# Two-operand elementwise operations moved from GpSimd to VectorE in a hybrid mLSTM and attention step

## The chip, the cores and the metric

The kernel runs on one core of one Trainium2 chip. The metric is the device time of one execution in microseconds, as the median of several runs.

## The reference

One layer of a decoder for a prompt of 1024 tokens and 32 sample tokens (8 sequences of 4), model width 1024, all in float32. Two branches read the same normalised input and are merged by gates:

```
h, gate = adaln_in(x, c, w_ada, b_ada, g_norm)          # rmsnorm(x) * (1 + scale) + shift
(mq, mk, mv, mi, mf, mo, mz, aq, ak, av, az, gm, ga) = split_in(h @ w_in)
y_m, C, n, m = mlstm_branch(mq, mk, mv, mi, mf, mo, mz, C0, n0, m0, b_i, b_f, g_mn)
q = partial_rope(aq, pos); k = partial_rope(ak, pos)
o = attn_prompt(q, k, v, sinks)                          # window 128, 8 heads, 2 key heads
y_a = o * silu(az)
u = sigmoid(gm) * (y_m @ w_mo) + sigmoid(ga) * (y_a @ w_ao)
x = x + gate * (u @ w_o)                                 # then a last rmsnorm
```

Inside the mLSTM branch, for each of 4 heads and each chunk of 128 tokens (b is the running sum of the log forget gates):

```
dmat = where(causal, b[:, None] - b[None, :] + ig[None, :], -inf)
s = (q @ k.T) * exp(dmat - m_hat[:, None])
num = s @ v + w_inter[:, None] * (q @ C)
h = num / max(abs(dot), exp(-m_hat))[:, None]
C_new = decay * C + (w_end * k).T @ v
```

and its output is multiplied by sigmoid(mo) * silu(mz). The sample tokens take the same layer with a state C0, n0, m0 of their own and cached keys and values.

## The kernel before

**Engines by name.** In the code V is VectorE (DVE in the profile), S is ScalarE (ACT), G is GpSimd (POOL); every load and store is issued on SyncE's queue (SP). V and S are wrappers that record each instruction, so that all their work, and TensorE's, has one helper line in the profile: L219 for V and S, L257 for products (`mm`), L262 for transposes (`tr`), L245 for transfers. G is the bare engine, so that its instructions carry the line of the code that issues them.

**Products.** A float32 product is three reduced-precision ones: an operand is split into hi (a cast, on ScalarE) and lo = raw - hi (a subtraction, on VectorE), and hi x hi, hi x lo and lo x hi are added in PSUM. Tokens are columns, in pieces of 384, 384 and 288 (1024 prompt and 32 sample tokens).

**Stages.** From 0 to about 60 us the input is loaded and normalised. To about 360 us follow the projections ("jobs"): attention queries, then for each mLSTM head its queries, keys and values (tiles g_aq, g_mq, g_mk, g_mv). Between their products TensorE is given pieces of side work by a planner that keeps a clock of estimated product times: attention units (scores sc, exponentials p, transposes pt, ScalarE's and VectorE's copies of them pT, output oT), the gate chain, and the heads in stages a to d. From 360 to 690 us come the gates' projections in 14 pairs of weights (8 `gate`, 2 `query_gate`, 4 `head_gate`), each pair by a scheme with seven block products instead of eight, for which sums of blocks of the input (`sum_blocks`, tiles hb) and of the weights (`Pair.first_sums`, `Pair.split`, tiles wr_ and ws) are made ahead. Splits of weights (tiles wh_, wl_) are made two products ahead. Then follow the two branches' output products (g_w_ao, g_w_mo) and the last product (fo).

**Rope** (line 737). A tile x of queries or keys becomes x * cos + shuffle(x) * sin: VectorE shuffles and multiplies by sin (ropet), the other product is a second instruction, VectorE adds both (aqr, krr).

**Head stage a** (lines 1029 and 1032). Tile et is loaded with rows of the gate chain and the causal mask is added; tile qw is loaded with weights and multiplied by the head's queries hq. A memset of vn's last column (line 1022) is on GpSimd too, with ScalarE's weighting hv <- vn behind it.

**Other names.** f3den, f3v, f3r_ and f2...: the small chain (3 or 2 columns) that normalises a head's chunk outputs, ending in a scaling of et; mx, nmx, den: the softmax's maximum, its negative, its denominator; gs: the sample tokens' head output times a weight; row: a row of the gate chain; t1 to t4 with h and l: splits of the hb sums; bx, by, bz, bw: PSUM banks of the block products, evacuated into gt, zt or hg; ho: a head's or query's output that hg or zt is multiplied by (lines 1416 and 1392); Cs: the sample states, decayed at line 1174; sU: the products that update them; uqv, ukv: loaded attention operands.

**What sets the order.** TensorE's order is fixed by hand: each product is made to follow the one before it (`in_order`). VectorE and ScalarE are ordered by hand in the beginning only; from there on a scheduler orders VectorE, ScalarE, GpSimd and SyncE by its own estimates. Each engine then takes its instructions strictly in that order, each waiting for its own operands.

## Time and profile before

| | |
|---|---|
| median of 3 runs | 882.72 us (882.6 to 884.04) |
| profiled execution | 881.87 us |
| its span | 880.1 us |
| TensorE (PE) busy | 844.3 us, 96% |
| VectorE (DVE) busy | 546.8 us, 62% |
| ScalarE (ACT) busy | 383.9 us, 44% |
| GpSimd (POOL) busy | 200.6 us, 23%, 206 instructions |
| HBM traffic | 106.02 MB read, 39.51 MB written |

Times are microseconds from the start of the span unless marked ns. A row of a timeline gives the start, the duration, the engine, the line, the operation, the tile written, the tiles read, the shape and a count; in brackets stands the engine's idle time just before it and what ended it. A row of a group gives busy time in all and the mean of one instruction in ns. An idle engine costs time only if something that sets the end waits for it.

### The profile page before, as it was taken

How to read it: one execution, taken by the hardware profiler on the slowest of the kernel's cores; microseconds unless marked ns; L12 is line 12 of the kernel's file. 1: busy time of each engine (PE TensorE's matmuls, PEld its weight loads, DVE VectorE, ACT ScalarE, POOL GpSimd, SP SyncE). 2: the span in 40 equal slices, each digit the busy share in tenths (PEclk: the TensorE clock that was granted, in tenths of full speed). 3: DMA queues.
4: the chain of work that ended last, by engine and by line, in shares of the span. 5: the costliest groups of instructions: out<-in, count | busy, mean ns of one | idle time of the engine just before them, and what ended most of it. 6: DMA issues, size and time to landing. Idle time of an engine off the chain costs nothing. (4 is left out here: it accounts for less than half of the span.)

```text
span 880.1 us, 15550 instructions
## 1 busy us (share of the span) xinstructions
PE 844.3 (96%) x5304; PEld 715.1 (81%) x5304; DVE 546.8 (62%) x1512; ACT 383.9 (44%) x984; POOL 200.6 (23%) x206
## 2 busy tenths in 40 slices
PE   6899999999999889999999999999999999999996
PEld 2689988888889878788878877777788999987775
DVE  4877673444748876444754554567756667747785
ACT  4762344445445455555545444444344333223231
POOL 0002320000024432223312223355443302220000
PEclk9899999999999999999999999999999999999998
DMA  9996437374567443445444344554424789453421
GB/s 312 369 332 199 117 123 266 106 239 128 172 176 225 141 141 109 128 150 149 100 137 119 107 128 122 155 160 134 132 85 140 256 279 304 141 156 106 145 79 48
DMA packets 114347, 145.55 MB, mean 165 GB/s; under 512 B 27068, under 2 KB 72508, under 8 KB 114236
## 3 DMA queue, kind: packets, MB, share of 16 engines
q1 hardware_dynamic: 114268, 144.56, 52.0%
q8 instruction: 42, 0.69, 0.3%
q14 instruction: 37, 0.30, 0.1%
HBM read 106.02 MB, written 39.51 MB: 165 GB/s over the span
## 5 line engine op out<-in xcount | busy, mean ns | idle before, releaser
L257 PE MATMUL g_w_ao<-ya,wh_w_ao 128*128 128x384 f32 (+1 forms) x192 | 45.5, 322 | 0.9 <-ACT bw L219 0.5
L257 PE MATMUL g_w_mo<-ym_l,wh_w_mo 128*128 128x384 f32 (+1 forms) x192 | 45.7, 323 | 0.0
L219 ACT ACTIVATE p<-p,nmx 128x256 f32<-128x256 f32 (+1 forms) x64 | 31.0, 485 | 30.1 <-DVE nmx L219 30.1
L219 DVE CUSTOM_DVE_ANT_0 p<-sc,cst,sink 128x256 f32<-128x256 f32 (+1 forms) x64 | 26.1, 462 | 21.6 <-PE sc L257 21.5
L257 PEld LDWEIGHTS g_w_ao<-ya,wh_w_ao 128*128 128x128 f32 x192 | 33.4, 188 | 1.6 <-ACT bw L219 1.0
L219 ACT ACTIVATE fjk<-rows_l 128x512 bf16<-128x512 f32 (+2 forms) x19 | 11.6, 609 | 51.7 <-DVE rows_l L219 25.8
L257 PEld LDWEIGHTS g_w_mo<-ym_l,wh_w_mo 128*128 128x128 f32 x192 | 33.5, 188 | 0.0
L257 PE MATMUL g_mk<-h_h,wh_mk 128*128 128x384 f32 (+1 forms) x96 | 33.4, 348 | 0.0
L257 PE MATMUL g_aq<-h_h,wh_aq 128*128 128x384 f32 (+1 forms) x96 | 33.0, 344 | 0.0
L257 PE MATMUL g_mv<-h_h,wh_mv 128*128 128x384 f32 (+1 forms) x96 | 33.0, 344 | 0.0
L257 PE MATMUL g_mq<-h_h,wh_mq 128*128 128x384 f32 (+1 forms) x96 | 32.5, 338 | 0.0
L257 PE MATMUL g_aq<-h_l,wh_aq 128*128 128x384 f32 (+1 forms) x96 | 31.6, 329 | 0.0
L257 PE MATMUL g_aq<-h_h,wl_aq 128*128 128x384 f32 (+1 forms) x96 | 31.6, 329 | 0.0
L257 PE MATMUL g_mk<-h_l,wh_mk 128*128 128x384 f32 (+1 forms) x96 | 31.6, 329 | 0.0
L257 PE MATMUL g_mk<-h_h,wl_mk 128*128 128x384 f32 (+1 forms) x96 | 31.4, 327 | 0.0
L257 PE MATMUL g_mv<-h_h,wl_mv 128*128 128x384 f32 (+1 forms) x96 | 31.0, 323 | 0.0
L257 PE MATMUL g_mq<-h_l,wh_mq 128*128 128x384 f32 (+1 forms) x96 | 31.0, 323 | 0.0
L257 PE MATMUL g_mq<-h_h,wl_mq 128*128 128x384 f32 (+1 forms) x96 | 31.0, 323 | 0.0
L257 PE MATMUL g_mv<-h_l,wh_mv 128*128 128x384 f32 (+1 forms) x96 | 31.0, 323 | 0.0
L257 PE MATMUL g_w_mo<-ym_l,wl_w_mo 128*128 128x384 f32 (+1 forms) x96 | 31.0, 323 | 0.0
L257 PE MATMUL g_w_ao<-ya,wl_w_ao 128*128 128x384 f32 (+1 forms) x96 | 30.8, 321 | 0.0
L737 POOL TENSOR_TENSOR aq<-aq,cos 128x384 f32<-128x384 f32 (+1 forms) x12 | 15.0, 1252 | 46.1 <-DVE ropet L219 40.2
(1321 smaller groups left out, 2746.1 us busy)
## 6 DMA issues: line engine op xcount, KB each, us to landing
x<-xT SPq DMA_DIRECT2D x16, 256.0 KB, 5.2
early_h<-w_ada SPq DMA_DIRECT2D x8, 512.0 KB, 7.7
hD<-x SPq DMA_DIRECT2D x16, 256.0 KB, 4.8
adar_ga<-w_ada SPq DMA_DIRECT2D x16, 256.0 KB, 5.4
wr_ga<-w SPq DMA_DIRECT2D x16, 256.0 KB, 3.1
hb<-hD SPq DMA_DIRECT2D x16, 256.0 KB, 6.5
wr_gm<-w SPq DMA_DIRECT2D x16, 256.0 KB, 3.3
taD<-gt SPq DMA_DIRECT2D x16, 256.0 KB, 3.4
```

The source lines that it names most:

```text
L219: ins = f(*args, **kw)
L257: in_order(nc.tensor.matmul(out, lhsT, rhs, start=start, stop=stop, skip_group_check=more))
L737: G.tensor_tensor(x, x, cs[0], op=ALU.mult)
```

## The change

Every `G.tensor_tensor` in six places becomes a `V.tensor_tensor` with the same operands: rope's cosine product, the mask and the weighting of head stage a, the decay of the sample states, the block sums, the weight sums, and the last multiplication of the two kinds of gated outputs. That is 139 instructions.

```diff
 def rope(x, cs, n, dst, dram, c0):
-            G.tensor_tensor(x, x, cs[0], op=ALU.mult)
+            V.tensor_tensor(x, x, cs[0], op=ALU.mult)
...
 def stage_a(p):
-                G.tensor_tensor(et[:, :m], et[:, :m], cmask.unsqueeze(1).to_broadcast((128, m, 128)), op=ALU.add)
+                V.tensor_tensor(et[:, :m], et[:, :m], cmask.unsqueeze(1).to_broadcast((128, m, 128)), op=ALU.add)
...
-                G.tensor_tensor(qw[:, :m], qw[:, :m], q[:, :w].rearrange("p (c e) -> p c e", e=128), op=ALU.mult)
+                V.tensor_tensor(qw[:, :m], qw[:, :m], q[:, :w].rearrange("p (c e) -> p c e", e=128), op=ALU.mult)
...
 for c, b, m in zip(Cs, bs, ns_):
-                G.tensor_tensor(c[:, :m], c[:, :m], sxb[:, h, 2, b].unsqueeze(2).to_broadcast((128, m, 129)), op=ALU.mult)
+                V.tensor_tensor(c[:, :m], c[:, :m], sxb[:, h, 2, b].unsqueeze(2).to_broadcast((128, m, 129)), op=ALU.mult)
...
 def sum_blocks():
-                G.tensor_tensor(b22, b22, b12, op=ALU.subtract)
+                V.tensor_tensor(b22, b22, b12, op=ALU.subtract)
...
 def first_sums(self):
-                G.tensor_tensor(self.raw["s1"], self.raw[1, 0], self.raw[1, 1], op=ALU.add)
+                V.tensor_tensor(self.raw["s1"], self.raw[1, 0], self.raw[1, 1], op=ALU.add)
...
 def split(self, i):
-                    G.tensor_tensor(r[0, 1], r[0, 1], r[0, 0], op=ALU.subtract)
+                    V.tensor_tensor(r[0, 1], r[0, 1], r[0, 0], op=ALU.subtract)
...
 query_gate.evac
-                G.tensor_tensor(t, t, self.held.pop((c, th)), op=ALU.mult)
+                V.tensor_tensor(t, t, self.held.pop((c, th)), op=ALU.mult)
...
 head_gate.evac
-                    G.tensor_tensor(z, z, self.held.pop(th), op=ALU.mult)
+                    V.tensor_tensor(z, z, self.held.pop(th), op=ALU.mult)
```

The other three block sums and two first sums change in the same way. Left on GpSimd are its memsets, small copies of sample columns (line 976), the lo parts of ya and of half of wo (lines 1700 and 1723) and the output additions of line 1244.

TensorE's order stays the same, row for row. VectorE's order takes in the new instructions where the scheduler puts them. In rope, on VectorE (the last query piece), the cosine product stands behind the sine product, and a weight split comes ahead of the addition:

```order
 L219 STREAM_SHUFFLE ropet<-aq 128x288
 L219 TENSOR_TENSOR ropet<-ropet,sin_545 128x288
-L219 TENSOR_TENSOR den<-den,nmx 128x4
+L219 TENSOR_TENSOR aq<-aq,cos_544 128x288
+L219 TENSOR_TENSOR wl_mk_1_1517<-wr_mk_1_1286,wh_mk_1_1516 128x512
 L219 TENSOR_TENSOR aqr<-aq,ropet 128x256
 L219 TENSOR_TENSOR qpad<-aq,ropet 64x8x4 x2
-L219 TENSOR_TENSOR wl_mk_1_1517<-wr_mk_1_1286,wh_mk_1_1516 128x512
+L219 TENSOR_TENSOR den<-den,nmx 128x4
```

So a cosine product is now followed by the addition on the same engine; the softmax's den moves behind it.

On VectorE near the first block sums (hb_0, at 262 us in the profile before), two score passes (the rows with ISA write mx) stand ahead:

```order
 L219 ISA p_3167,mx<-sc_6_1_3170,cst,sink 128x256
 L219 ISA mx 128x1
-L219 SCALAR_TENSOR_TENSOR fsden<-sns 32x1
+L219 TENSOR_TENSOR hb_0_3134<-hb_0_3134,hb_0_3130 128x512
 L219 TENSOR_SCALAR nmx<-mx 128x4
 L219 TENSOR_TENSOR nmx<-sink,mx 128x4
+L219 TENSOR_TENSOR hb_0_3130<-hb_0_3130,hb_0_3128 128x512
+L219 SCALAR_TENSOR_TENSOR fsden<-sns 32x1
```

The first sum, which reads a tile that a load has to bring, stands ahead of nmx now.

On VectorE near the second block sums (hb_1, at 281 us), where gs stood near the end of the f3 chain:

```order
+L219 TENSOR_TENSOR hb_1_3376<-hb_1_3376,hb_1_3382 128x512
 L219 RECIPROCAL f3den<-f3den 128x3
+L219 TENSOR_TENSOR hb_1_3380<-hb_1_3380,hb_1_3376 128x512
 L219 TENSOR_TENSOR f3v<-f3den 128x3
+L219 TENSOR_TENSOR t4l_3244<-hb_0_3132,t4h_3243 128x512
+L219 COPY mk_3494<-g_mv_3424 128x384
+L219 TENSOR_TENSOR et<-et,cst 128x256
+L219 TENSOR_TENSOR qw<-qw,hq_2_3160 128x256
+L219 TENSOR_SCALAR gs<-sty_3513,vec 128x32
 L219 TENSOR_TENSOR f3v<-f3v,mssq 128x3
```

t4l, the mk copy and gs move ahead of the rest of the chain (they leave its end), and et and qw come in just ahead of gs.

GpSimd's queue at the same place, before:

```order
L1279 TENSOR_TENSOR hb_1_3382<-hb_1_3382,hb_1_3378 128x512
L1280 TENSOR_TENSOR hb_1_3378<-hb_1_3378,hb_1_3376 128x512
L1330 TENSOR_TENSOR ws_4245<-wr_gm_0_3951,wr_gm_1_3953 128x512
L1282 TENSOR_TENSOR hb_1_3376<-hb_1_3376,hb_1_3382 128x512
L1283 TENSOR_TENSOR hb_1_3380<-hb_1_3380,hb_1_3376 128x512
L1022 MEMSET vn 128x2
L1029 TENSOR_TENSOR et<-et,cst 128x256
L1032 TENSOR_TENSOR qw<-qw,hq_2_3160 128x256
L1022 MEMSET vn 128x3
```

and after, from the copy of sample columns ahead of it:

```order
L976 COPY ks<-mk_3389 128x32
L1022 MEMSET vn 128x2
L1022 MEMSET vn 128x3
L976 COPY vs<-mk_3662 128x32
L976 COPY qs<-mk_3944 128x32
```

The memset of vn, which ScalarE waits for, has no sum ahead of it any more.

More of the change, by code (lines that the diff above doesn't have):

```diff
@@ L1278, in sum_blocks @@
                     block_tiles(n, k)
-                G.tensor_tensor(b22, b22, b12, op=ALU.subtract)
-                G.tensor_tensor(b12, b12, b11, op=ALU.subtract)
+                V.tensor_tensor(b22, b22, b12, op=ALU.subtract)
+                V.tensor_tensor(b12, b12, b11, op=ALU.subtract)
                 yield 2.5, ""
-                G.tensor_tensor(b11, b11, b22, op=ALU.add)
-                G.tensor_tensor(b21, b21, b11, op=ALU.subtract)
+                V.tensor_tensor(b11, b11, b22, op=ALU.add)
+                V.tensor_tensor(b21, b21, b11, op=ALU.subtract)
                 t1.append(b12)
@@ L1329, in first_sums @@
                 self.raw["s1"] = raw_tile("ws1")
-                G.tensor_tensor(self.raw["s1"], self.raw[1, 0], self.raw[1, 1], op=ALU.add)
-                G.tensor_tensor(self.raw[1, 0], self.raw[0, 0], self.raw[1, 0], op=ALU.subtract)
-                G.tensor_tensor(self.raw[0, 0], self.raw["s1"], self.raw[0, 0], op=ALU.subtract)
+                V.tensor_tensor(self.raw["s1"], self.raw[1, 0], self.raw[1, 1], op=ALU.add)
+                V.tensor_tensor(self.raw[1, 0], self.raw[0, 0], self.raw[1, 0], op=ALU.subtract)
+                V.tensor_tensor(self.raw[0, 0], self.raw["s1"], self.raw[0, 0], op=ALU.subtract)
             def split(self, i):
```

## The prediction

> **What bounds the kernel now.** I read the page's shares first, then the chain, then TensorE's waits, and last the timelines around those waits.

> ```profile
> PE 844.3 (96%) x5304; PEld 715.1 (81%) x5304; DVE 546.8 (62%) x1512; ACT 383.9 (44%) x984; POOL 200.6 (23%) x206
> PE 31%; issue 1%; DVE 1%; POOL 1%; DMA 1%; SPq 0%; ACT 0%; POOLq 0%; DVEq 0%
> ```

> TensorE is busy 96% of the span, and GpSimd (POOL) makes 1% of the chain that ended last. The change takes no instruction from TensorE, so all it can win is TensorE's waits and what they do to its clock. TensorE's waits (line, tile, engine waited for: us in total, times, longest), without those of the first and last 60 us and three under 0.7 us:

> ```profile
> PE bw L257 <- ACT bw L219: 2.8, 2, 1.6
> PE sc L257 <- ACT uqv L219: 2.6, 1, 2.6
> PE pt L262 <- DVE gs L219: 2.5, 1, 2.5
> PE sU L257 <- DVE Cs L219: 2.5, 4, 0.9
> ...
> PE pt L262 <- DVE row L219: 1.9, 1, 1.9
> ...
> PE smp L257 <- ACT pT L219: 0.9, 1, 0.9
> ...
> PE g_w_ao L257 <- POOL ya L1700: 0.4, 1, 0.4
> ```

> Together 13.6 us. To these come two stretches at half clock (columns: window, length, TensorE busy, granted clock), the first behind the wait for row, the second behind that for uqv:

> ```profile
> 115.77:119.18 3.41, 3.41 (x13) 0.50 0.00 0
> 327.39:330.81 3.42, 3.42 (x11) 0.50 0.22 77
> ```

> Half of 3.41 us, 1.7 us, is the most that each can cost; I take 1.6. So 13.6 + 3.2 = 16.8 us (1.9%) is the ceiling of a gain here.

> **What moves.** 139 two-operand instructions leave POOL for VectorE (DVE): 88 of 512 columns, 26 of 384, 8 of 387, 8 of 256, 4 of 258, 5 of 288, some 62,700 columns, or 122 x 512. DVE's price for such a product, and a DVE group of the same size that runs beside POOL:

> ```profile
> L219 DVE TENSOR_TENSOR wl_mk<-wr_mk,wh_mk 128x512 fp32r<-128x512 f32 x8 | 5.5, 690 | 2.3 <-ACT wh_mk L219 2.2
> L219 DVE SCALAR_TENSOR_TENSOR hg<-hg,hg 128x512 f32<-128x512 f32 x8 | 11.4, 1423 | 0.2
> ```

> 122 x 0.69 = 84 us of new DVE work. Against it stands what DVE loses beside POOL: 8 x (1.42 - 0.69) = 5.9 us in the hg group alone. It shows best on three-column instructions:

> ```profile
> 281.80 1.29 POOL L1279 TENSOR_TENSOR hb<-hb,hb 128x512 f32<-128x512 f32 x1 [3.33 <-DVE f3den L219]
> 281.91 1.20 DVE L219 TENSOR_TENSOR f3v<-f3den 128x3 f32<-128x3 f32 x1
> 288.24 0.10 POOL L1022 MEMSET vn<- 128x2 f32 x1
> 288.37 0.70 ACT L219 ACTIVATE hv<-vn,wend 128x129 f32<-128x129 f32 x2 [6.07 <-POOL vn L1022]
> 289.87 0.16 DVE L219 TENSOR_TENSOR f3r_w<-f3r_w,f3v 128x3 f32<-128x3 f32 x1
> 291.22 0.24 DVE L219 TENSOR_SCALAR gs<-sty,vec 128x32 f32<-128x32 f32 x1
> ```

> f3v, started behind hb, ends with hb, near 283.1; alone such an instruction takes 0.16 us. [...] From rows, DVE ends between 547 (all 84 us given back) and 547 + 84 - 6 = 625 us; I take the middle, 585 (66%). DVE does not become full, so the question is place by place, in DVE's order.

> 1. **Rope, 107 to 115 us.** DVE waits for POOL's cosine product, and TensorE for DVE's copy `row`, which stands behind it:

> ```profile
> 111.17 1.08 POOL L737 TENSOR_TENSOR aq<-aq,cos 128x288 f32<-128x288 f32 x1 [2.27 <-DMA qD<-aqr]
> 112.30 0.42 DVE L219 TENSOR_TENSOR aqr<-aq,ropet 128x256 f32<-128x256 f32 x1 [0.71 <-POOL aq L737]
> 114.92 0.55 PE L262 MATMUL pt<-cst,p 128*128 128x128 f32 x3 [1.87 <-DVE row L219]
> ```

> On DVE this product costs 0.69 x 288/512 = 0.4 us and the wait of 0.71 goes: 0.3 us earlier, and 0.35 more from the rope before it. The stall shrinks by 0.65 to 1.2 us. Waits of that length elsewhere (bw, 1.2 and 1.6) had no half-clock stretch behind them, so its 1.6 us go too: -2.2.

> 2. **Block sums hb_1, 281 to 291 us** (rows above). POOL's five products hold back the `vn` memset, that holds ACT for 6.07 us, and they stretch DVE's chain, behind which stands `gs`. After, the sums cost DVE 5 x 0.69 = 3.5 us, but et, qw and gs stand ahead of most of that chain. From 281.05: products 3.5, two C updates 0.7, small ones 0.65, t4l 0.7, the mk copy 0.55, et and qw 0.9: gs starts near 288 instead of 291.2, before TensorE comes to pt: -2.5.

> 3. **Block sums hb_3, 321 to 340 us.** POOL waits for the tile's DMA beside DVE; after the change DVE itself waits, with the attention's `nmx` behind it:

> ```profile
> 321.90 0.16 DVE L219 TENSOR_TENSOR f2v<-f2den 128x2 f32<-128x2 f32 x1
> 325.06 1.26 POOL L1279 TENSOR_TENSOR hb<-hb,hb 128x512 f32<-128x512 f32 x1 [3.86 <-DMA hb<-hD]
> 325.34 0.62 ACT L219 CAST t2h<-hb 128x512 fp32r<-128x512 f32 x1 [2.68 <-DMA qD<-mk]
> 328.05 2.73 DVE L219 TENSOR_SCALAR et<-et,f2den,f2r_y 128x128 f32<-128x128 f32 x2
> 333.04 0.17 DVE L219 TENSOR_SCALAR nmx<-mx 128x4 f32<-128x4 f32 x1
> L219 DVE CUSTOM_DVE_ANT_0 p<-sc,cst,sink 128x256 f32<-128x256 f32 (+1 forms) x64 | 26.1, 462 | 21.6 <-PE sc L257 21.5
> ```

> DVE arrives at 321.9 and blocks 3.2 us, but the two et scalings, 2.73 us under POOL, stand behind nmx now. From 325.06: four sums 2.8, t2l and t4l 1.4, four score passes 1.85, small ones 1: nmx near 332.1, 0.9 us earlier. The wait of smp for pT (0.9) goes: -0.9. The 2.6 us for uqv stay, since ACT ahead of it waits for a DMA, and so does the half clock behind them.

> 4. **Gate evacuation, 439 us.**

> ```profile
> 438.01 0.35 DVE L219 TENSOR_SCALAR et<-et,f3den,f3r_y 128x128 f32<-128x128 f32 x1
> ...
> 438.87 1.56 DVE L219 TENSOR_SCALAR et<-et,f3den,f3r_y 128x128 f32<-128x128 f32 x2
> 439.03 1.32 POOL L1339 TENSOR_TENSOR wr_ga<-wr_ga,wr_ga 128x512 f32<-128x512 f32 x1 [1.67 <-DVE wl_pgate__5310 L219]
> ```

> The weight sum costs the two et 0.9 us, and with them gt, ACT's bw copy and TensorE (1.6) are late. After, DVE pays 0.69 for it, and et and qw just ahead no longer stretch two small instructions: -0.6, between -1.6 and 0.

> 5. **ya, 691 us.** The last ya product stood on POOL behind an hg product:

> ```profile
> 689.13 1.45 POOL L1416 TENSOR_TENSOR hg<-hg,ho 128x512 f32<-128x512 f32 x1 [0.63 <-DVE hg L219]
> ```

> With hg gone from POOL's queue ya starts up to 1.4 us earlier: -0.4. (Six ya, eight wo_l and six output adds stay on POOL; the diff does not touch them.)

> 6. **Losses.** DVE takes its instructions in order, so a sum that waits for a DMA holds all behind it. The worst is hb_0, with `nmx` next:

> ```profile
> 262.79 0.08 DVE L219 DVE_READ_ACCUMULATOR2_ANT mx<- 128x1 f32 x1
> 264.75 0.15 DVE L219 TENSOR_SCALAR nmx<-mx 128x4 f32<-128x4 f32 x1
> 266.61 1.29 POOL L1279 TENSOR_TENSOR hb<-hb,hb 128x512 f32<-128x512 f32 x1 [8.73 <-DMA n_s<-Cs]
> 271.01 0.91 ACT L219 ACTIVATE p<-p,den 128x256 f32<-128x256 f32 x2 [2.92 <-DVE den L219]
> ```

> DVE comes to it at 262.9 and can start near 266.5; nmx moves to 267.3, 2.5 us later. What covers it: ACT's four exponentials then end 2.5 us later, at 269.7, while the step after them waits now until 271.0 for a den that stands in DVE's stretched chain. I charge 0.3, between 0 and 2.5. et and qw hold DVE in the same way near 198 us (0.4) and 245 (0.2). The decay of Cs brings DVE three products a head in the sample stage, where TensorE waits 0.6 us a head for Cs: they run 0.2 us apiece faster or slower than now, -2.4 to +2.4 in all; I take +0.5. Weight splits fall behind et and qw once or twice; they are made two products ahead, and these cover them: 0; without that cover the wait is that of an et for its DMA, up to 4 us. A few stores change places with loads on SP's queue; their readers come a product later: 0 to 0.5, taken as 0. Sum +1.4, at worst some +5.

> Sum: -2.2 - 2.5 - 0.9 - 0.6 - 0.4 + 1.4 = -5.2 us. The profiled execution takes 881.87 (span 880.1), which makes 876.7; the median of the runs shown, 882.72, lies 0.85 higher: 877.5.

> **Rivals.**

> - *TensorE alone sets the time; no change.* Each wait above ends on the next thing: at 114.9 on the score passes, at 291 on ACT's pT, at 340 on the softmax. For it: 96% busy, and the sum is 0.6% of the time. Against it: gs, row and Cs are DVE's with POOL in front of it. 881 to 884.5.

> - *DVE blocked at its head: slower.* One mechanism, the in-order wait for a DMA that POOL took until now; it decides where the 2.5 us at hb_0 and the 3.2 us at hb_3 exceed the softmax's lead over TensorE's pt. With no lead at both: 2.5 + 3.2 and two half-clock stretches, +8.9, less places 1, 4, 5 and half of 2 (4.4): 887.2. Against it: TensorE idles little there, so its leads are mostly long:

> ```profile
> 180.00:360.00 180.00, 172.47 (x1275) 154.64 (x1274) 117.03 (x362) 93.51 (x284) 44.59 (x55) 0.99 0.56 168
> ```

> - *The clock stays.* A wait's length alone does not bring the half clock: 2.5 us before 291.5 did not, 1.9 before 114.9 did. If the first stretch stays, 879.1. [...]

> - *More goes than I count.* uqv's 2.6 us and its stretch go too: 877.5 - 4.2 = 873.3. Against it: ACT's DMA wait at 325.34.

> **How the numbers follow.** Forecast with either clock case (875.5 to 880.9) 0.57; more goes (below 875.5) 0.11; no change 0.18; blocked DVE 0.14. A measurement of this kernel tells some 0.2% (1.8 us) from no change: faster 0.68, same 0.18, slower 0.14. The predicted time is **877.5 us**. The range leaves out the end of the last rival (0.05) and the blocked DVE: 873.5 to 884.5; the forecast's own is 875.5 to 880.9.

> **What will show it.** Right: DVE near 585 us; the f3v chain at 0.16 us apiece; no TensorE wait for gs, and the one for row near 1.2 us with no half clock behind it; none for ya. Wrong: TensorE waits for ACT's yt, pT or p near 200 or 265 to 275 us while DVE stands ahead of hb, et or qw for a DMA; new half-clock stretches; weight splits later than their products.

## The result and the profile after

The changed kernel takes 869.66 us (median of 4 runs, 868.19 to 870.61) against 882.66 us for the kernel before (median of 4 runs, 880.67 to 884.04): a ratio of 0.9853, with an interval of 0.9829 to 0.9877. That is 13.0 us faster where 5.2 were forecast, and below the range's end of 873.5. The direction and most places were right; the step that failed is place 3, with the wait for uqv.

The page of the profiled execution after (870.61 us, span 868.8; shares of the span, then the chain that ended last):

```profile
PE 842.2 (97%) x5304; PEld 712.6 (82%) x5304; DVE 569.3 (66%) x1651; ACT 385.0 (44%) x984; POOL 33.3 (4%) x67
PE 56%; DVE 2%; ACT 1%; issue 0%; DVEq 0%
```

139 instructions went from POOL (206 to 67) to DVE (1512 to 1651), and POOL is gone from the chain. DVE rose by 22.5 us only. In this trace the 139 add 75.1 us to its busy time (569.3 with them, 494.2 without them; their own times add up to 87.6 us, but neighbouring instructions overlap: at 264.94, below, nmx starts 0.08 us before the sum ahead of it ends), and the other 1512 take 494.2 us instead of 546.8: 52.6 us came back. TensorE's waits after, the same view as before:

```profile
PE sU L257 <- DVE Cs L219: 3.7, 4, 1.4
...
PE bw L257 <- ACT bw L219: 2.0, 2, 1.2
...
PE sc L257 <- ACT uqv L219: 0.2, 1, 0.2
PE pt L262 <- DVE row L219: 0.2, 1, 0.2
PE smp L257 <- ACT pT L219: 0.2, 1, 0.2
```

No wait is left for gs (2.5), none for ya (0.4); row fell from 1.9 to 0.2, uqv from 2.6 to 0.2, smp from 0.9 to 0.2; sU grew by 1.2. TensorE's busy time within the stretch that held the long waits, which was 172.47 of 180 us:

```profile
180.00:360.00 180.00, 176.37 (x1301) 158.41 (x1298) 117.93 (x416) 99.42 (x301) 4.49 (x19) 1.00 0.59 172
```

Its granted clock is 1.00 now, and between 60 and 860 us no stretch at half clock is left, where there were two.

**An account by place.** TensorE runs the same 5304 instructions in the same order in both kernels, so the start of one instruction in both traces gives a lag, and the steps of the lag say where the time went. With before's times:

| where (before's time) | step, us | what |
|---|---|---|
| first 60 us | +0.5 | loads of x and of the gates; -2.3 to +2.2 in the runs below |
| 112 to 119, place 1 | -3.2 | wait for row -1.67, half clock -1.53 |
| 256, sample stage | +0.8 | wait for Cs |
| 291.5, place 2 | -2.7 | wait for gs |
| 326.7, place 3 | -4.0 | wait for uqv -2.43, its half clock -1.54 |
| 332 and 340, place 3 | -1.4 | waits for mx and pT, small steps between |
| 442.8, place 4 | -0.8 | wait for bw |
| 577.9, sample stage | +0.5 | wait for Cs |
| 691.4, place 5 | -0.6 | wait for ya |
| the rest | -0.4 | steps under 0.3 us each |
| all | -11.3 | 881.87 to 870.61 us |

The profile after is the slowest of its four runs, and the first 60 us (-2.3 to +2.2) and single waits (up to 1.6 us, in the second execution of the kernel before) differ between runs, so the 1.7 us between -11.3 and the medians' -13.0 are not put to a place.

**Place 1.** Timeline after: the addition of one rope (107.82), then the next rope with its product by cos, then TensorE's transpose behind row:

```profile
107.82 0.56 DVE L219 TENSOR_TENSOR aqr<-aq,ropet 128x384 f32<-128x384 f32 x1
...
110.67 0.45 DVE L219 TENSOR_TENSOR aq<-aq,cos 128x288 f32<-128x288 f32 x1
111.15 0.42 DVE L219 TENSOR_TENSOR aqr<-aq,ropet 128x256 f32<-128x256 f32 x1
...
113.78 0.55 PE L262 MATMUL pt<-cst,p 128*128 128x128 f32 x3 [0.20 <-DVE row L219]
```

**Place 2.** The f3 chain after, gs and the transpose that waited for it:

```profile
282.34 0.15 DVE L219 TENSOR_TENSOR f3v<-f3den 128x3 f32<-128x3 f32 x1
...
284.15 0.24 DVE L219 TENSOR_SCALAR gs<-sty,vec 128x32 f32<-128x32 f32 x1
...
286.53 0.88 PE L262 MATMUL pt<-cst,p 128*128 128x128 f32 x6
```

f3v takes 0.15 us instead of 1.20, and gs is done 2.1 us before TensorE comes to pt.

**Place 3, the step that was wrong.** Before, ACT's cast `t2h` waited 2.68 us for a store (qD<-mk), and I took that as a DMA's own time. SyncE's queue and DVE before:

```profile
306.38 1.62 POOL L1280 TENSOR_TENSOR hb<-hb,hb 128x512 f32<-128x512 f32 x1
306.77 1.25 DVE L219 TENSOR_SCALAR nmx<-mx 128x4 f32<-128x4 f32 x1
...
317.37 2.81 SPq L245 DMA_DIRECT2D hb<-hD  x4
320.85 0.32 SPq L245 DMA_DIRECT2D qD<-mk  x1
```

and after, with the cast and TensorE's score product behind it:

```profile
301.46 0.16 DVE L219 TENSOR_SCALAR nmx<-mx 128x4 f32<-128x4 f32 x1
...
309.06 3.92 SPq L245 DMA_DIRECT2D hb<-hD  x4
...
315.60 0.32 SPq L245 DMA_DIRECT2D qD<-mk  x1
...
317.47 0.62 ACT L219 CAST t2h<-hb 128x512 fp32r<-128x512 f32 x1
...
319.58 1.13 PE L257 MATMUL sc<-ukv,uqv 64*128 64x256 f32 x6 [0.21 <-ACT uqv L219]
```

Before, the four hb_3 loads (1 MB) were issued right ahead of the small store: 0.67 us lie between the end of their issue and the store's. By the landing events of the trace the last load landed at 324.90 and the store at 325.27, 4.42 us after its issue; t2h started at 325.34. After, the gap is 2.62 us, the last load landed at 316.08, and the store at 317.39, 1.79 us after its issue; t2h started at 317.47, after a wait of 0.04 us. The loads are issued 8.3 us sooner (3.6 of it against TensorE, whose lag is 4.7 there), since the work ahead of them on SyncE's queue is: before, `nmx` at 306.77 took 1.25 us instead of 0.16 beside POOL's hb_2 sums, and behind it came ACT's exponentials, a copy of mk and the store of that copy, which stands ahead of the loads. The scheduler also put that copy of mk ahead of the scaling by den, so the timeline does not say how much of the 8.3 us each of the two brought.

**The loss at hb_0 came as told, and was covered.** After, DVE, then ACT:

```profile
264.33 0.69 DVE L219 TENSOR_TENSOR hb<-hb,hb 128x512 f32<-128x512 f32 x1 [3.35 <-DMA hb<-hD]
264.94 0.16 DVE L219 TENSOR_SCALAR nmx<-mx 128x4 f32<-128x4 f32 x1
...
267.85 0.91 ACT L219 ACTIVATE p<-p,den 128x256 f32<-128x256 f32 x2
```

DVE stands 3.35 us ahead of the sum, with nmx behind it. The exponentials begin late (nmx 2.1 us later against TensorE), yet the scaling by den starts at 267.85 instead of 271.01, 1.3 us sooner against TensorE: den stood behind three instructions of one column that took 1.14 to 1.15 us beside POOL's sums; now they take 0.15, and den stands ahead of them. TensorE is busy 20.00 of 20 us from 260 to 280 in both kernels.

### The profile page after: what moved, and what is told of

Its sections match the earlier page's. It is cut to its first block, busy times and chain, and to the rows that moved or that the text cites. A ratio compares the mean times of both kernels' runs of the same rounds, so it can differ in the third digit from the quotient of the medians.

```text
span 868.8 us, 15418 instructions
## 1 busy us (share of the span) xinstructions
PE 842.2 (97%) x5304; PEld 712.6 (82%) x5304; DVE 569.3 (66%) x1651; ACT 385.0 (44%) x984; POOL 33.3 (4%) x67
## 4 chain that ended last, share of the span: by engine, by line
PE 56%; DVE 2%; ACT 1%; issue 0%; DVEq 0%
PE fo L257 10%; PE bw L257 9%; PE bx L257 9%; PE by L257 9%; PE g_w_mo L257 5%; PE g_w_ao L257 5%; PE bz L257 4%; PE smp L257 2%; PE n L257 1%; PE S L257 0%; PE U L257 0%; PE sn L257 0%; PE smpo L257 0%; PE ty L262 0%; DVE rows_l L219 0%
## 5 line engine op out<-in xcount | busy, mean ns | idle before, releaser
L257 PE MATMUL g_w_ao<-ya,wh_w_ao 128*128 128x384 f32 (+1 forms) x192 | 45.3, 321 | 0.5 <-ACT bw L219 0.5
L257 PE MATMUL g_w_mo<-ym_l,wh_w_mo 128*128 128x384 f32 (+1 forms) x192 | 45.7, 323 | 0.0
L219 ACT ACTIVATE p<-p,nmx 128x256 f32<-128x256 f32 (+1 forms) x64 | 30.9, 484 | 22.6 <-DVE nmx L219 22.6
L219 DVE CUSTOM_DVE_ANT_0 p<-sc,cst,sink 128x256 f32<-128x256 f32 (+1 forms) x64 | 26.4, 462 | 15.0 <-PE sc L257 15.0
L219 ACT ACTIVATE fjk<-rows_l 128x512 bf16<-128x512 f32 (+2 forms) x19 | 11.6, 609 | 51.3 <-DVE rows_l L219 25.5
L257 PEld LDWEIGHTS g_w_ao<-ya,wh_w_ao 128*128 128x128 f32 x192 | 33.3, 188 | 1.0 <-ACT bw L219 1.0
L257 PEld LDWEIGHTS g_w_mo<-ym_l,wh_w_mo 128*128 128x128 f32 x192 | 33.5, 188 | 0.0
L257 PE MATMUL g_mv<-h_h,wh_mv 128*128 128x384 f32 (+1 forms) x96 | 33.0, 344 | 0.0
L257 PE MATMUL g_mk<-h_h,wh_mk 128*128 128x384 f32 (+1 forms) x96 | 32.8, 341 | 0.0
L257 PE MATMUL g_mq<-h_h,wh_mq 128*128 128x384 f32 (+1 forms) x96 | 32.5, 338 | 0.0
L257 PE MATMUL g_aq<-h_h,wh_aq 128*128 128x384 f32 (+1 forms) x96 | 32.3, 336 | 0.0
L257 PE MATMUL g_mv<-h_h,wl_mv 128*128 128x384 f32 (+1 forms) x96 | 31.0, 323 | 0.0
L257 PE MATMUL g_mq<-h_h,wl_mq 128*128 128x384 f32 (+1 forms) x96 | 31.0, 323 | 0.0
L257 PE MATMUL g_mk<-h_l,wh_mk 128*128 128x384 f32 (+1 forms) x96 | 31.0, 323 | 0.0
L257 PE MATMUL g_mq<-h_l,wh_mq 128*128 128x384 f32 (+1 forms) x96 | 31.0, 323 | 0.0
L257 PE MATMUL g_aq<-h_l,wh_aq 128*128 128x384 f32 (+1 forms) x96 | 31.0, 323 | 0.0
L257 PE MATMUL g_mv<-h_l,wh_mv 128*128 128x384 f32 (+1 forms) x96 | 31.0, 323 | 0.0
L257 PE MATMUL g_mk<-h_h,wl_mk 128*128 128x384 f32 (+1 forms) x96 | 31.0, 323 | 0.0
L257 PE MATMUL g_w_mo<-ym_l,wl_w_mo 128*128 128x384 f32 (+1 forms) x96 | 31.0, 323 | 0.0
L257 PE MATMUL g_aq<-h_h,wl_aq 128*128 128x384 f32 (+1 forms) x96 | 31.0, 323 | 0.0
L257 PE MATMUL g_w_ao<-ya,wl_w_ao 128*128 128x384 f32 (+1 forms) x96 | 30.8, 321 | 0.0
L219 DVE SCALAR_TENSOR_TENSOR u_h<-tgw_ao,g_w_ao 128x384 f32<-128x384 f32 (+1 forms) x24 | 12.4, 518 | 13.2 <-PE g_w_ao L257 13.0
```

Source lines behind the costliest of these rows:

```text
L219: ins = f(*args, **kw)
L257: in_order(nc.tensor.matmul(out, lhsT, rhs, start=start, stop=stop, skip_group_check=more))
```

## The experiments

Theory A of the expectations is the prediction's mechanism, with what the trace after added: DVE's small instructions take longer beside POOL's two-operand ones (f3v 1.20 us beside a block sum before, 0.15 after); TensorE's waits for row and gs follow from that at once, and the wait for uqv one step later, by way of SyncE's queue. Its rivals stand in the texts themselves. Ratios are to the kernel before on the same chip in the same series (881.89 us there for the first four).

### The rope alone (15 of 139 instructions)

```diff
-            G.tensor_tensor(x, x, cs[0], op=ALU.mult)
+            V.tensor_tensor(x, x, cs[0], op=ALU.mult)
```

> Only rope's 15 cosine products go to VectorE. Theory A (the gain is made at separate places, each by its own group): TensorE's wait for row at 114.9 us falls from 1.87 us to 0.7 or less and the half-clock stretch at 115.8 us (1.5 to 1.7 us) goes, nothing else changes: 2.5 to 3.3 us faster than before. Theory B (the gain needs GpSimd empty everywhere, since the groups hand their delays on to each other): under 1 us, and the stretch at half clock stays or moves.

Measured: 879.71 us, ratio 0.997 (0.9953 to 0.9988). The timeline at place 1:

```profile
115.47 0.55 PE L262 MATMUL pt<-cst,p 128*128 128x128 f32 x3 [0.20 <-DVE row L219]
```

The wait falls from 1.87 to 0.20 us and no half clock follows: -3.2 us by the lag, the whole of place 1. The medians give 2.2 us (1.1 to 4.1 by the interval), a little under the 2.5 to 3.3 expected. uqv (2.7) and gs (2.7) stay. The wait for bw at 442 shrinks from 1.57 to 0.89 though nothing near it was changed; this returns below.

### The block sums alone (16 instructions)

```diff
-                G.tensor_tensor(b22, b22, b12, op=ALU.subtract)
-                G.tensor_tensor(b12, b12, b11, op=ALU.subtract)
+                V.tensor_tensor(b22, b22, b12, op=ALU.subtract)
+                V.tensor_tensor(b12, b12, b11, op=ALU.subtract)
...
-                G.tensor_tensor(b11, b11, b22, op=ALU.add)
-                G.tensor_tensor(b21, b21, b11, op=ALU.subtract)
+                V.tensor_tensor(b11, b11, b22, op=ALU.add)
+                V.tensor_tensor(b21, b21, b11, op=ALU.subtract)
```

> Only the 16 block sums hb go to VectorE. Theory A: TensorE's wait for gs (2.5 us) goes, and with the sums off GpSimd at 305 to 311 us the softmax, ScalarE's mk copy and SyncE's loads of hb_3 come 2 to 3 us earlier against TensorE, so that the store of mk lands before ScalarE wants its buffer: the wait for uqv (2.6 us), its half-clock stretch (1.7) and most of the wait for pT (0.9) go too: 7 to 9 us faster. Theory B (the wait for uqv is a DMA's own, as the prediction had it, and was cured by something else in the change): 3 to 4 us faster, the wait for uqv still 2 us or more.

Measured: 873.0 us, ratio 0.9898 (0.9869 to 0.9927). Sixteen instructions bring nearly 9 us. gs -2.70, uqv -2.43 and its half clock, mx and pT about -1.4; the wait for row and its half clock stay. The queue, the cast and the product at place 3:

```profile
311.40 3.03 SPq L245 DMA_DIRECT2D hb<-hD  x4
...
316.49 0.32 SPq L245 DMA_DIRECT2D qD<-mk  x1
...
318.35 0.62 ACT L219 CAST t2h<-hb 128x512 fp32r<-128x512 f32 x1
...
320.53 1.13 PE L257 MATMUL sc<-ukv,uqv 64*128 64x256 f32 x6 [0.21 <-ACT uqv L219]
```

2.06 us between the loads and the store, which lands 1.78 us after its issue. So moving the block sums is enough to take the wait for uqv away.

### The weight sums alone (56 instructions)

```diff
-                G.tensor_tensor(self.raw["s1"], self.raw[1, 0], self.raw[1, 1], op=ALU.add)
+                V.tensor_tensor(self.raw["s1"], self.raw[1, 0], self.raw[1, 1], op=ALU.add)
...
-                    G.tensor_tensor(r[0, 1], r[0, 1], r[0, 0], op=ALU.subtract)
+                    V.tensor_tensor(r[0, 1], r[0, 1], r[0, 0], op=ALU.subtract)
```

(lines 1331 and 1332 likewise)

> Only the 56 sums of weights go to VectorE. Theory A: TensorE's wait for bw at 442.8 us shrinks by about 0.8 us, the rest stays: 0.5 to 1 us faster. Theory B (what matters is how much work GpSimd has in all; these are 40% of it): 4 us or more faster.

Measured: 882.39 us, ratio 1.0017 (1.0002 to 1.0031): no gain, where A had a small one. bw -0.73 at 442, but Cs at 578 +0.49, and the wait for gs is 3.6 instead of 2.5 us, now with half clock behind it. The largest group of moved instructions is worth nothing; how much work leaves POOL does not set the gain.

### The rest alone (masks, weightings, decay, gating: 52 instructions)

```diff
-                G.tensor_tensor(et[:, :m], et[:, :m], cmask.unsqueeze(1).to_broadcast((128, m, 128)), op=ALU.add)
+                V.tensor_tensor(et[:, :m], et[:, :m], cmask.unsqueeze(1).to_broadcast((128, m, 128)), op=ALU.add)
```

(lines 1032, 1174, 1392 and 1416 likewise)

> Masks, weightings, state decays and the two kinds of gated outputs (52 instructions) go to VectorE. Theory A: the wait for ya (0.4 us) goes, part of bw's wait perhaps, and the waits for Cs grow by 1.2 us in all: within 1 us of before. Theory B (GpSimd's amount of work counts): 4 us or more faster.

Measured: 883.83 us, ratio 1.0026 (1.0006 to 1.0047): 1.9 us slower, where A had it within 1 us. Waits of TensorE:

```profile
PE sU L257 <- DVE Cs L219: 4.2, 4, 2.0
PE pt L262 <- DVE gs L219: 2.9, 1, 2.9
PE n L257 <- DVE mx L219: 2.6, 1, 2.6
...
PE sc L257 <- ACT uqv L219: 0.2, 1, 0.2
```

uqv is cured here too, which neither theory had (the store is issued 1.51 us behind the loads and lands at 323.72, 1.90 us later), and a wait of 2.6 us for mx, which was 0.2, stands in its place 6 us later. Taking uqv's wait away brought nothing here, where POOL still has the block sums; how DVE's chain behind it runs beside them (1.11 to 1.25 us for instructions of 0.16) is shown by the run with the whole change but for the block sums, below.

### The hb_3 loads issued behind the store

Everything stays on POOL; only the last block load is issued after the transfer that follows it.

```diff
-                if k < 3:
+                if k < 2:
                     nxt = load(k + 1)
...
+                    if k == 2 and n == "t3":
+                        nxt = load(3)
```

> The kernel before, all sums on GpSimd; only the four loads of hb_3 are issued one transfer later on SyncE's queue, behind the store of mk that ScalarE's t2h waits for. Theory A (that store lands late because 1 MB of loads is queued just ahead of it): it lands some 1.9 us after its issue instead of 4.4, TensorE's wait for uqv falls from 2.6 us to under 0.5 and its half-clock stretch goes; part comes back at TensorE's wait for mx, since hb_3 lands later: 2 to 4 us faster. Theory B (GpSimd's sums set that wait): the wait for uqv stays at 2 us or more, no faster.

Measured: 881.93 us, ratio 1.0004 (0.9983 to 1.0024).

```profile
318.73 0.32 SPq L245 DMA_DIRECT2D qD<-mk  x1
319.16 1.81 SPq L245 DMA_DIRECT2D hb<-hD  x4
...
322.19 0.61 ACT L219 CAST t2h<-hb 128x512 fp32r<-128x512 f32 x1
...
324.89 0.49 ACT L219 ACTIVATE mk<-g_mk 128x384 f32<-128x384 f32 x1 [2.09 <-DVE t2l L219]
...
325.69 1.13 PE L257 MATMUL sc<-ukv,uqv 64*128 64x256 f32 x6 [3.63 <-ACT uqv L219]
```

The first half of A holds: with the loads behind it, the store landed at 320.66, 1.93 us after its issue, and the cast waits for no DMA. The second, that the time falls, does not: the mk copy, which stands between t2h and uqv on ACT in the kernel before too, now waits 2.09 us for DVE's t2l, and TensorE's wait grows to 3.63. The scheduler changed a few orders on ACT and DVE and the cast and the copy have other waits than before, so this run does not price the store alone.

### GpSimd writes, but reads nothing

All 139 operations are left out; in place of each, GpSimd sets the operation's output twice to a constant, so the hand-overs of that output between engines stay, and the order nearly so; a memset does not wait for the second operand.

```diff
-                G.tensor_tensor(b22, b22, b12, op=ALU.subtract)
+                G.memset(b22, 1.0); G.memset(b22, 1.0)
```

(the other lines of the change likewise)

> The kernel before with each of the 139 moved operations left out and two memsets of its output put in its place, on GpSimd: the same waits from engine to engine and a similar time on GpSimd (some 1.2 us for 512 columns), but nothing read from SBUF by it. Theory A (most of the gain is GpSimd's reads no longer holding VectorE up): the three-column instructions at 282 to 289 us take 0.16 us again, VectorE is busy some 50 us less (near 495), the waits for gs and for uqv go, rope's wait for row stays above 1 us: 6 to 10 us faster. Theory B (the gain is the wait from engine to engine, one queue less): VectorE still waits for GpSimd as before, under 3 us faster.

Measured: 872.43 us, ratio 0.9905 (0.9882 to 0.9928; 881.45 us before in this series). The page, and DVE beside a pair of memsets:

```profile
PE 841.1 (97%) x5304; PEld 712.4 (82%) x5304; DVE 502.5 (58%) x1512; ACT 385.4 (44%) x984; POOL 156.5 (18%) x345
```

```profile
277.79 1.11 POOL L1330 MEMSET ws<- 128x512 f32 x2
...
278.11 0.16 DVE L219 TENSOR_TENSOR f3v<-f3den 128x3 f32<-128x3 f32 x1
278.65 0.16 DVE L219 TENSOR_TENSOR f3v<-f3v,mssq 128x3 f32<-128x3 f32 x1 [0.39 <-ACT mjk L219]
```

With the same instructions and nearly the same order DVE is busy 502.5 us instead of 546.8, and its two-operand three-column operations take 0.16 us while POOL works. The waits for gs and uqv go as A had it; the one for row goes too, which A did not expect. So f3v took 1.20 us beside a POOL instruction that reads two tiles (the kernel before) and 0.16 beside one that only writes. The stretching is not confined to two inputs: nmx, with one, took 1.25 us beside a block sum (above). A pair of memsets is also shorter than the operation it stands for (0.90 us for 384 columns against 1.34), so a part of the gain, that at row above all, may be POOL's own time. A new wait, 2.4 us for hg1z at 673 us, is the largest step by which this run lies behind the changed kernel.

### The decay of Cs left on GpSimd

The changed kernel with line 1174 as before:

```diff
-                V.tensor_tensor(c[:, :m], c[:, :m], sxb[:, h, 2, b].unsqueeze(2).to_broadcast((128, m, 129)), op=ALU.mult)
+                G.tensor_tensor(c[:, :m], c[:, :m], sxb[:, h, 2, b].unsqueeze(2).to_broadcast((128, m, 129)), op=ALU.mult)
```

> The changed kernel, but the 12 decays of the sample states stay on GpSimd. Theory A (places are separate): TensorE's waits for Cs fall from 3.7 us to 2.5 in all, the rest is as in the changed kernel: some 1.2 us faster than that one, 12 to 14 us faster than before. Theory B (two-operand work on GpSimd beside VectorE costs more than it saves, wherever it is): not faster than the changed kernel.

Measured: 871.9 us, ratio 0.99 (0.9882 to 0.9919): not faster than the changed kernel (0.9853), as B had it, though nothing here shows B's reason.

```profile
PE sU L257 <- DVE Cs L219: 3.8, 4, 1.4
```

The wait for Cs stays at 3.8 us (3.7 after, 2.5 before), so the decay is not what lengthened it: A was wrong here. The single runs put it elsewhere: the growth at 256 us came with the rest (sU 1.29 there) and the one at 578 with the weight sums (1.43) and with the rest (2.00). Other work that now stands in DVE's order ahead of Cs may be the reason; no run shows which.

### The kernel before, once more

> The kernel before, unchanged, for a second profile of it. Theory A: the waits of TensorE between 60 and 860 us are the same to 0.1 us. Where one differs (the wait for bw at 442.8 us, 1.57 us, came out at 0.89 in the run with only rope moved, which changed nothing near it), that one differs from execution to execution, and the change has no part in it. Theory B: bw's wait is 1.5 us or more again, and every group but the block sums shortens it.

Measured: 883.25 us in one execution.

```profile
PE pt L262 <- DVE gs L219: 2.9, 1, 2.9
...
PE sc L257 <- ACT uqv L219: 2.2, 1, 2.2
PE n L257 <- DVE mx L219: 1.8, 1, 1.8
```

```profile
293.00:296.41 3.41, 3.41 (x16) 3.41 (x15) 1.38 (x4) 0.62 (x1) 0.00 (x0) 0.50 0.63 167
```

The same program shows uqv at 2.2 instead of 2.6, gs at 2.9 instead of 2.5 and mx at 1.8 instead of 0.2, while row is 1.87 again; so A's first half, that they are the same to 0.1 us, is wrong at places 2 and 3. The half clock moved as well: here it stands behind gs (the window above, granted clock 0.50) and none behind uqv. So 1.5 us that the account puts to place 3 belonged to place 2 in this execution, and single waits there differ by up to 1.6 us; what the block sums cost at both places together is surer than its parts. The wait for bw at 442 came out at 1.50 again, as B had it.

### The rope and the block sums (31 instructions)

The diffs of the first two experiments together. The kernel before takes 881.38 us in this series and in the three after it.

> Only rope's 15 and the block sums' 16 operations go to VectorE, 31 of 139. Theory A (separate places that add up: 3.2 us at row, 8.2 at gs, uqv and pT): 10.5 to 12.5 us faster than before, as fast as the whole change within 1 us; TensorE's waits for Cs stay at 2.5 us in all, that for ya at 0.4. Theory B (GpSimd must be empty for the gain): half of it or less, 6 us.

Measured: 869.66 us, ratio 0.9865 (0.9838 to 0.9892). Waits of TensorE:

```profile
PE sU L257 <- DVE Cs L219: 2.5, 4, 0.9
PE bw L257 <- ACT bw L219: 2.2, 2, 1.2
```

31 of the 139 instructions bring the time of the whole change (0.9853, 0.9829 to 0.9877). Between the two profiles the other 108 bring 0.55 us at ya and cost 1.26 at Cs; the wait for bw is shorter in both (0.96 and 0.78).

### The rope, the block sums and the head gating

Line 1416 as well, as in the diff of the change.

> As the run with rope and block sums, and the 8 last multiplications of the heads' outputs (hg) on VectorE too. Theory A: TensorE's wait for ya (0.4 us) goes as well, the waits for Cs do not grow: some 0.5 us faster than without it, 11 to 13 us faster than before. Theory B: it adds a wait for Cs of 0.5 us, no difference.

Measured: 869.99 us, ratio 0.9869 (0.9839 to 0.9898). The wait for ya is gone (-0.55 us by the lag at 691) with Cs still at 2.5, but in time it cannot be told from the one above: this attempt at a version better than both kernels gives no more than the change.

### The whole change but for the block sums

```diff
-                V.tensor_tensor(b22, b22, b12, op=ALU.subtract)
-                V.tensor_tensor(b12, b12, b11, op=ALU.subtract)
+                G.tensor_tensor(b22, b22, b12, op=ALU.subtract)
+                G.tensor_tensor(b12, b12, b11, op=ALU.subtract)
```

(lines 1282 and 1283 likewise)

> The changed kernel, but the 16 block sums stay on GpSimd. Theory A: VectorE's f3 chain is held up again by them, TensorE waits 2.5 to 3.6 us for gs and for uqv or mx together 2 to 3 us, with a half-clock stretch behind one or both: 5 to 9 us slower than the changed kernel, 3 to 7 us faster than before. Theory B (with the rest of the work gone, GpSimd's sums no longer meet VectorE's chain): within 2 us of the changed kernel.

Measured: 878.68 us, ratio 0.9967 (0.9945 to 0.9989). uqv is cured here as well, and the stall comes back for mx. POOL's sum, DVE's chain beside it, and TensorE:

```profile
323.24 1.28 POOL L1279 TENSOR_TENSOR hb<-hb,hb 128x512 f32<-128x512 f32 x1 [1.30 <-DVE f2v L219]
323.30 1.25 DVE L219 TENSOR_SCALAR f2r_y<-f2v 128x2 int32<-128x2 int32 x1
...
324.79 1.11 DVE L219 TENSOR_TENSOR f2r_w<-f2r_y 128x2 f32<-128x2 f32 x1
...
332.12 0.46 PE L257 MATMUL n<-vn,et 128*128 128x129 f32 x2 [2.69 <-DVE mx L219]
```

Four instructions of two columns take 1.11 to 1.25 us instead of 0.16 beside the four sums, and mx stands behind them. By the medians of two series this is 9.0 us slower than the changed kernel, by the two ratios 10, at the end of A's 5 to 9 or just past it: the block sums are some 9 to 10 us of the change's 13.

### The block sums with a larger load ahead of the store

The block sums alone, and three extra transfers (393 KB each, memory to memory) issued around the hb_3 loads, so that the store finds a full queue again.

```diff
+                if k == 2:
+                    spare = dp.tile([128, 3, 768], F32, name="spare")
+                    for j in range(3):
+                        dma(spare[:, j], mD[NH - 1][0][:, 0:768])
```

> The run with only the block sums moved, and three copies of 393 KB from HBM to HBM that nobody reads, two ahead of the loads of hb_3 and one behind them, just ahead of the store of mk. Theory A (the store that ScalarE's t2h waits for lands late when megabytes are queued just ahead of it): it lands 4 us or more after its issue instead of 1.8, ScalarE waits 2 us or more before t2h, TensorE waits 1.5 us or more for uqv: 2 to 6 us slower than that run. Theory B (a store's landing does not depend on what is queued ahead of it): within 1 us of that run.

Measured: 876.2 us, ratio 0.9943 (0.9926 to 0.996).

```profile
317.35 0.32 SPq L245 DMA_DIRECT2D qD<-mk  x1
...
319.94 0.62 ACT L219 CAST t2h<-hb 128x512 fp32r<-128x512 f32 x1 [0.77 <-PE oT L257]
...
321.38 1.13 PE L257 MATMUL sc<-ukv,uqv 64*128 64x256 f32 x6 [0.21 <-ACT uqv L219]
```

The store landed at 323.20, 5.85 us after its issue instead of 1.78 and 0.34 us behind the last extra transfer (322.86): with more queued ahead, it landed later. But the cast does not wait for that store here (its wait of 0.77 us is for TensorE), so uqv's wait did not come back, against the expectation. The time is in A's range all the same, 3.2 us over the block sums alone by the medians and 4.0 by the ratios, but by another way: in the lag against that run, product n (it waits 1.8 us for f2r_w) and smp (0.9 again) make most of it, with DVE ahead of its first hb_3 sum for 2.91 us, until the last load landed (321.85).

## Why the prediction was wrong

- **Place 3, the step that failed.** "The 2.6 us for uqv stay, since ACT ahead of it waits for a DMA, and so does the half clock behind them." Both went: -2.43 and -1.54, 4.0 of the 6.1 us by which the profiled difference (-11.3) passes the forecast (-5.2). (In the second execution of the kernel before that half clock stood behind gs, so its place varies.) The row named a store, and I took its landing for fixed. It is not. In all 14 profiles the store landed 1.8 to 1.9 us after its issue, or, where a transfer queued ahead of it had not landed by then, 0.3 to 0.4 us behind that one: 4.42 us after its issue in the kernel before (4.67, 4.24 and 3.77 with the rope alone, the weight sums alone and in the second execution), 1.78 to 1.90 with the block sums or the rest moved. The distance in issue is not enough to tell it: with the decay left on GpSimd it is 0.58 us, and the store landed 2.28 us after its issue, 0.38 behind the last load. In every profile with the long wait, t2h begins as the store lands. So what counts is how early the loads of hb_3 land, and after the change that is 4.2 us earlier against TensorE. The rival that had it (873.3, 0.11) was the nearest of all, and its chance was too low. The runs with the block sums alone show that moving them takes this wait away; the rest alone takes it away too, but there the wait for mx comes in its place. That the landing follows from the queue ahead is shown by the extra transfers (5.85 us after its issue against 1.78) and by the loads moved behind the store (1.93 against 4.42); that TensorE's time follows from it alone is shown by neither, since orders and waits changed with them.
- **Place 1, mis-sized: -2.2 against -3.2.** The mechanism was right, and the rope alone shows it. The stall fell by 1.67 us, beyond the 0.65 that were counted. Against TensorE (0.53 us later there) the additions of the four ropes up to this point, at 98.82, 104.89, 108.93 and 112.30 before, are 0.9, 1.25, 1.64 and 1.68 us earlier: the lead is built up by the ropes ahead, of which I counted only the third (0.35), and the last, for which I had 0.3, adds almost nothing. The half clock went, as predicted (-1.53).
- **Place 2, right: -2.5 against -2.70.** The f3 chain, gs and the block sums as the cause are all as told, though gs starts even earlier (284.15, which is 286.1 by the kernel before's TensorE, not near 288).
- **Place 3, n and smp: -0.9 against -1.4.** Right to half a microsecond, but with luck: the block of 3.2 us that I had DVE pay at hb_3 did not come. Its first sum starts at 316.53 without a wait, since the loads had landed at 316.08; the path to nmx was another than the one I added up.
- **Place 4: the number came, its cause is not shown.** -0.6 against -0.8. But bw's wait at 442 is 1.39 to 1.59 us in the kernel before (twice), with the block sums alone and with the moved load, and 0.8 to 1.1 in the others, the rope alone among them, whose change lies 325 us away. The weight sum beside it cannot be the only cause; what sets it stays open.
- **Place 5, right: -0.4 against -0.6.** The head gating takes ya's wait away by itself.
- **Losses: +1.4 against +1.3, right in sum and wrong in its parts.** hb_0 (0.3) and the et at 198 and 245 (0.6) cost nothing; Cs cost 1.3 instead of 0.5, and not by the decay. The rival of a blocked DVE did not come: at hb_0 the block was there, but den came sooner all the same, and at hb_3 there was none.
- **DVE's load, 585 us against 569.3.** The 139 cost 75.1 us and not 84, and 52.6 us came back where the middle of my bounds had 46. That all 84 us would be given back, the lower bound, is shown by no run.
- **The clock.** Both stretches went with their waits: the granted clock is 1.00 from 112.36 to 119.18 us after, and over 60 to 860 us. The rival in which the first one stays did not come in the changed kernel; with the weight sums or the rest alone, new stretches did come (behind waits of 3.6 us for gs with the weight sums, and of 2.9 for gs, 2.6 for mx and 2.0 for Cs with the rest; the clock granted with the rest was 0.50 from 291.83 to 295.24 and from 332.79 to 336.20).

## What to carry to other kernels

A DMA that a trace names as the last to arrive is a cause only if its landing would be the same without the change (here it came 4.42 us after its issue before, and 1.79 after): look at what its queue carried just before it and what released that. Small VectorE operations that take several times their usual length beside GpSimd (here 1.11 to 1.25 us against 0.16) mark the instructions worth moving; here 31 of 139, those in front of a chain that TensorE waits for, brought a gain that cannot be told from the whole, and 56 others brought none. And the waits that a change makes are to be sought one step behind the ones that it removes, since a cured wait shows the next (uqv, then mx).

## What the runs showed of the hardware

**A partly idle step of 3.41 us was followed by half clock.** In the kernel before, the stretches at half clock start at 27.02, 115.77, 327.39 and 873.53 us, that is 26, 62 and 160 steps of 3.413 us apart. The stretches between 60 and 850 us of all profiles are 3.41 us long and lie on such a grid within each execution; with the rest alone two start at 291.83 and 332.79, 12 steps apart. The second of these (TensorE busy, granted clock 0.50):

```profile
332.79:336.20 3.41, 3.41 (x17) 3.41 (x16) 1.07 (x8) 2.94 (x13) 0.00 (x0) 0.50 0.08 23
```

**The small store landed behind the loads queued ahead of it.** It took 1.78 us with the loads ahead of it landed (the block sums alone), 4.42 us in the kernel before, 0.37 us behind the last load, and 5.85 us behind the loads and the extra transfers, 0.34 us behind the last of these.

**One-input operations of VectorE are stretched too.** Beside GpSimd's block sums f2r_y<-f2v, 128x2 with one input, took 1.25 us (the change without the block sums), and 0.16 to 0.17 us in the changed kernel.
